# Retention with its group norm finished on GpSimd and ScalarE, other PSUM slots, and the modulation rows spread anew

## The chip, the cores and the metric

The kernel runs on one NeuronCore of a Trainium2 chip. Its engines work in parallel, each through its own instructions in order, and wait for each other through semaphores: TensorE (PE in the profile) multiplies matrices, VectorE (DVE) and ScalarE (ACT) work on tiles of 128 partitions, GpSimd (POOL) does small and odd work, and SyncE (SP) issues most of the DMAs. [...] The metric is the device time of one execution in microseconds (us). The kernel before takes 2175.5 us (median of 3 runs, 2174.44 to 2175.85).

## The reference

One decoder block on a sequence of 1024 tokens of width 1024, all in float32. What matters here is the retention: four heads, each with keys of 256 and values of 512, in chunks of 128 tokens, whose output is normed over its 512 values and gated.

```python
def step(state, inp):
    qi, ki, vi = inp
    s = jnp.einsum('bhid,bhjd->bhij', qi, ki) * inner_decay[None]
    o = (jnp.einsum('bhij,bhje->bhie', s, vi)
         + jnp.einsum('bhid,bhde->bhie', qi, state) * q_decay[None, :, :, None])
    state = (state * chunk_decay[None, :, None, None]
             + jnp.einsum('bhjd,bhje->bhde', ki * k_decay[None, :, :, None], vi))
    return state, o
...
mu = jnp.mean(ro, axis=-1, keepdims=True)
var = jnp.mean(jnp.square(ro - mu), axis=-1, keepdims=True)
ro = ((ro - mu) * lax.rsqrt(var + GN_EPS)).transpose(0, 2, 1, 3).reshape(B, S, RET_V_W)
ro = (ro * gn_g.astype(jnp.float32) + gn_b.astype(jnp.float32)).astype(h.dtype)
ret_out = (jax.nn.silu(rg) * ro) @ w_ret_out
...
mod = jax.nn.silu(c) @ w_ada[l] + b_ada[l]
sh1, sc1, g1, sh2, sc2, g2 = jnp.split(mod, 6, axis=-1)
```

Around it stand a dilated sliding-window attention, the merge of both branches, a projection, a squared-ReLU MLP and the norms. The vector mod scales and shifts the normed inputs (6 x 1024 values).

## The kernel before

All matmuls run in a split form. Each operand is cut into a high and a low half (`wh`, `wl`: ACT casts to the high half, DVE subtracts it to get the low one), and `mm3` (L203) issues three matmuls of 128x512 for each product: low weight by high input (L207), high by low (L209), high by high (L211). The first one of a product thus needs the low half of the weight.

The order of the instructions is written out by hand; there is no scheduler. `Steps` walks a list of steps. Each step has loads (weights or rows that go through a ring of three raw tiles, `wraw`) and a body. A body gets a function `ahead`, which prepares the loads of the next step: for a weight that is the ACT cast and the DVE subtraction of `split_w` (L197, L198), for a modulation row the DVE product of `mod_prep`. When the body calls it decides where these instructions stand in the order of ACT and DVE.

The stages that matter, in order:

1. `queries_keys` (about 180 to 600 us) runs 22 pairs of projections (`PAIRS`), each as seven block products (`ORDER`). The last six pairs have no rotation to do and are called light here. From product 116 on, `mod_turn` (L1248) computes rows of the modulation: it multiplies a row of `w_ada` with the conditioning vector and sums it (L1252, DVE, 128x1024), in a ring of two tiles (`cossin`) that SP refills (L1254). 32 rows are done this way, one in 16/7 calls; the calls go on in the next stage.
2. `values` (600 to 712 us) computes what is left of the retention's values. Its results go through the same three raw tiles (`vo`) and out by SP (`vd<-vo`, L1371).
3. The retention (712 to 980 us): 32 steps, `chunk(h, c)`, for four heads of eight chunks. The number g counts through. In each chunk PE computes, in this order, the state's update `kv` (six matmuls, not in chunk 7 of a head), some slices of a gate projection `rg` (below), the scores of the next chunk (`s_kt`: sT, and the transposed keys kT), the output `o` (from the state and from the scores), the transposes `oT` of the chunk before (`on_T`), and one more slice of `rg`.
   - DVE and ACT turn `kv` into the new state and its halves (L745, L749, L750), and sT and kT into the operands of the next chunk (sm, kh, kl and so on). kl, DVE's last but one of these, is what the next chunk's `kv` starts with.
   - `jit_qk` casts the queries and keys of chunk g + 2 on ACT (L616) and makes their low half on POOL (L617, 128x512).
   - The norm: DVE takes the statistics of `o` (bn_stats, L772, and L773), adds the epsilon (L774), POOL raises to the power -1/2 (L775), DVE multiplies with the decay (L776) and norms `o` to `onm` (L778).
   - `on_T` copies the transposes into `on` with four ACT copies.
   - `u_final` for the head before stands at the end of chunks 0 to 3 of heads 1 to 3: two ACT passes (L688) and one DVE product with the gate (L690), and the result out by SP.
4. A gate projection takes eight slices (one for each 128 of the contraction, six matmuls each). `RG` says how many slices each chunk gets, `rg_mm` issues them, `rg_out` applies Silu (L710). Three of a head's four gates are computed here, one comes from DRAM. The twelve weights are loads of the steps at c = 0, 2, 5.
5. The attention's first step, `att_step(0, 0)`, starts with a projection of keys (`ak`), whose weight is prepared by the last chunk's `ahead`.

`banks` divides PSUM: in the retention two gate pairs of two banks each (`ps_mm`) and four slots of one bank (`ps_s`), which kv, sT, kT, o and oT share.

## Time and profile before

| what | number |
|---|---|
| median of 3 runs | 2175.5 us |
| the profiled execution: its time | 2173.28 us |
| the profiled execution: its span, first to last instruction | 2171.3 us |
| mean granted TensorE clock | 0.999 |
| PE, DVE, ACT busy from 181 to 600 us, of 419 us | 419.0, 307.2, 123.3 |
| PE, DVE, ACT busy from 600 to 712 us, of 112 us | 108.8, 67.9, 46.4 |
| PE, DVE, ACT busy from 712 to 785 us, of 73 us | 71.2, 49.4, 34.9 |
| PE, DVE, ACT busy from 785 to 980 us, of 195 us | 194.9, 148.1, 105.8 |

How to read the lines of the profile that follow. A row of a group names the source line, the engine, the operation, out<-in by the program's names with the shapes, the count, then the busy time, the mean in ns, and the idle time of the engine before them with what ended it. A row of the timeline has the start in us from the span's start, the duration in us, then engine, line, operation, names and count; in brackets the idle time before it and who ended it. A row of waits names who waited for whom, the total in us, how often, and the longest. A row of stages has busy us (and instructions) of PE, its weight loads, DVE, ACT and POOL, then the granted clock, the DMA engines' share and GB/s. Matmuls of 128x512 last 0.39 us each but start every 0.226 us, so PE can lose some tenths of a us between two starts without an idle gap.

### The profile page before, as it was taken

Reading aid. Unit: us, or ns where it says so; the run is one execution under the profiler, and the core shown is the slowest. Engines: PE = TensorE matmul, PEld = TensorE weight load, DVE = VectorE, ACT = ScalarE, POOL = GpSimd, SP = SyncE. Lnnn points to the kernel's source line nnn. Section 1 sums busy time; section 2 is a strip of 40 time slices with the busy share of each in tenths; the row PEclk is TensorE's granted clock in tenths of the full one; section 3 lists DMA queues with packets and bytes.
Section 4 is the critical chain, followed back from the end, with each engine's and each line's share of the span. In section 5 each row is a group of like instructions: output and inputs, shape, how many; then the busy total and the mean of one; then the engine's idle time right before and its main releaser. Section 6 shows DMA issues by size and latency. Waiting matters only on the chain. (4 is left out here: it accounts for less than half of the span.)

```text
span 2171.3 us, 27289 instructions
## 1 busy us (share of the span) xinstructions
PE 2144.7 (99%) x10036; PEld 1782.4 (82%) x10036; DVE 1520.4 (70%) x2358; ACT 959.3 (44%) x1757; POOL 165.7 (8%) x199
## 2 busy tenths in 40 slices
PE   8999999999999999999999999999999999999998
PEld 6888888888887788888888888888778888888887
DVE  6886777777656677776667644677876665877855
ACT  5543322323334455556656625434454455533413
POOL 0001111100001112211110000001000000000003
PEclk9999999999999999999999999999999999999999
DMA  9859998835588744436877366653144435645322
GB/s 383 282 208 309 285 306 265 243 117 194 186 301 303 234 148 151 160 127 197 218 194 196 115 245 211 217 191 132 64 175 160 150 136 193 253 135 173 109 88 78
DMA packets 162674, 425.18 MB, mean 196 GB/s; under 512 B 28005, under 2 KB 55916, under 8 KB 159468
## 3 DMA queue, kind: packets, MB, share of 16 engines
q1 hardware_dynamic: 150264, 374.90, 48.3%
q0 software_dynamic: 9584, 48.24, 9.9%
q8 instruction: 79, 1.29, 0.2%
q10 hardware_dynamic: 2692, 0.30, 0.1%
q14 instruction: 55, 0.45, 0.1%
HBM read 324.13 MB, written 160.32 MB: 223 GB/s over the span
## 5 line engine op out<-in xcount | busy, mean ns | idle before, releaser
L207 PE MATMUL qap<-hh,qaw 128*128 128x512 f32 x264 | 102.7, 389 | 0.0
L209 PE MATMUL qap<-hl,qaw 128*128 128x512 f32 x264 | 102.7, 389 | 0.0
L211 PE MATMUL qap<-hh,qaw 128*128 128x512 f32 x264 | 102.7, 389 | 0.0
L617 POOL TENSOR_TENSOR j<-qk,j 128x512 fp32r<-128x512 f32 x32 | 42.8, 1338 | 454.8 <-ACT j L616 454.8
L2235 POOL TENSOR_TENSOR accnf<-accnf,sqnf 128x256 f32<-128x256 f32 (+1 forms) x18 | 16.6, 922 | 609.6 <-ACT sqnf L2231 609.6
L2339 ACT ACTIVATE a<-a 128x512 f32<-128x512 f32 x48 | 30.3, 631 | 72.8 <-DVE a L2338 71.3
L749 ACT CAST stateh<-state 128x512 fp32r<-128x512 f32 x54 | 32.9, 622 | 57.8 <-DVE state L745 55.7
L209 PEld LDWEIGHTS qap<-hl,qaw 128*128 128x128 f32 x264 | 49.5, 188 | 10.4
L211 PEld LDWEIGHTS qap<-hh,qaw 128*128 128x128 f32 x264 | 49.6, 188 | 10.3
L207 PEld LDWEIGHTS qap<-hh,qaw 128*128 128x128 f32 x264 | 49.5, 188 | 10.2
L2547 ACT CAST w2h<-w2s 128x512 fp32r<-128x512 f32 x36 | 22.4, 621 | 80.3 <-DVE w2s L2585 80.3
L264 DVE TENSOR_TENSOR fw<-w1r,fw 128x512 fp32r<-128x512 f32 x48 | 32.9, 688 | 33.6 <-ACT fw L254 33.6
L264 DVE TENSOR_TENSOR qaw<-wa,qaw 128x512 fp32r<-128x512 f32 x66 | 44.0, 687 | 9.4 <-ACT qaw L254 9.4
L2070 DVE TENSOR_TENSOR rwl<-rwl,rwh 128x1024 fp32r<-128x1024 f32 x25 | 30.2, 1221 | 29.0 <-ACT rwh L2100 29.0
L207 PE MATMUL fp<-h2h,fw 128*128 128x512 f32 x128 | 50.0, 390 | 0.0
L209 PE MATMUL fp<-h2l,fw 128*128 128x512 f32 x128 | 49.8, 389 | 0.0
L211 PE MATMUL fp<-h2h,fw 128*128 128x512 f32 x128 | 49.8, 389 | 0.0
L207 PE MATMUL roa<-rh,rwl 128*128 128x512 f32 x128 | 49.8, 389 | 0.0
L209 PE MATMUL roa<-rl,rwh 128*128 128x512 f32 x128 | 49.8, 389 | 0.0
L211 PE MATMUL roa<-rh,rwh 128*128 128x512 f32 x128 | 49.8, 389 | 0.0
L1603 ACT ACTIVATE P<-P,ng 128x128 f32<-128x128 f32 (+1 forms) x96 | 41.9, 438 | 17.6 <-DVE ng L1595 17.5
L292 DVE TENSOR_TENSOR qat<-qat,qap 128x512 f32<-128x512 f32 x22 | 15.1, 688 | 42.8 <-PE qap L211 35.8
(3089 smaller groups left out, 7187.8 us busy)
## 6 DMA issues: line engine op xcount, KB each, us to landing
cossin<-in_w_ada_dram SPq DMA_DIRECT2D x32, 512.0 KB, 3.5
v<-vd SPq DMA_DIRECT2D x32, 512.0 KB, 4.3
w1r<-in_w_ff_dram SPq DMA_DIRECT2D x32, 512.0 KB, 4.6
yt<-y POOLq DMA_DIRECT2D x24, 512.0 KB, 7.5
xsd<-as SPq DMA_DIRECT2D x24, 512.0 KB, 3.1
w2r<-in_w_ff2s_dram SPq DMA_DIRECT2D x24, 512.0 KB, 6.4
em<-in_w_ada_dram SPq DMA_DIRECT2D x16, 512.0 KB, 10.2
wrvs<-in_w_rv_dram POOLq DMA_DIRECT2D x16, 512.0 KB, 9.8
```

Of the source, the lines that this page charges most:

```text
L207: nc.tensor.matmul(o, wl, xh, start=first, stop=False, skip_group_check=skip)
L209: nc.tensor.matmul(o, wh, xl, start=False, stop=False, skip_group_check=skip)
L211: nc.tensor.matmul(o, wh, xh, start=False, stop=last, skip_group_check=skip)
L264: nc.vector.tensor_sub(t[:, 512:], src, fv(t[:, :512]))
L292: nc.vector.tensor_sub(u, u, b)
L617: nc.gpsimd.tensor_sub(t[:, 1], src, fv(t[:, 0]))
L749: nc.scalar.copy(sh1[:, i, :], st[:, i, :])
L1603: nc.scalar.activation(v, v, AF.Exp, bias=ng[:, blk:blk + 1], accum_out=st[:, g, blk, 2 + a:3 + a])
L2070: nc.vector.tensor_sub(lo, fv(lo), fv(hi))
L2235: (nc.vector if f == 7 else nc.gpsimd).tensor_add(G["acc", key], G["acc", key], sq)
L2339: nc.scalar.activation(o, o, AF.Relu)
L2547: nc.scalar.copy(hi, src)
```

## The change

- The norm's algebra: instead of the decay and its square (`CS_QD`, `CS_QD2`) the constants hold -1 and the epsilon divided by the decay's square. DVE adds that epsilon to the variance. POOL negates the mean, takes the power, and multiplies both. ACT applies scale and bias to `o` (one pass of 128x512 from PSUM) in place of DVE.
- `ahead(2)` of every chunk but the first moves from ahead of `s_kt` to behind the norm, and stands before `u_final`.
- PSUM in the retention: three gate halves of one bank (`ps_rg`) instead of two pairs of two, and five slots instead of four. The division of before comes back with the attention's first step.
- Each half of a gate has its own Silu, right behind the gate's last slice in `rg_mm`. The tiles of `on` are pairs of two, with two ACT copies instead of four.
- Head 3's slices are 4, 4, 4, 3, 3, 3, 3, 0. The weight of a gate is a load of the step in which its first slice stands.
- 22 modulation rows instead of 32 in `mod_turn`, one in 1.5 calls, so that all lie in the light pairs. The other ten are loads of the steps (0, 6), and (h, 4), (h, 5), (h, 6) of the heads 1 to 3.

```diff
-    def banks(single):
+    def banks(single, ret=False):
...
-        PS["n"] = 8 if single else 4
+        PS["n"] = 8 if single else 5 if ret else 4
...
+    def ps_rg(name):
+        return PS["p"].tile([P, 512], F32, tag="rg", bufs=3, name=name)
...
-            hd["on", h] = [etile(f"on{h}{e}") for e in range(4)]
+            hd["on2", h] = [R["p"].tile([P, 2, 1024], F32, tag="EO", bufs=4, name=f"on{h}{e}") for e in range(2)]
+            hd["on", h] = [hd["on2", h][e // 2][:, e % 2] for e in range(4)]
...
-        for e in range(4):
-            nc.scalar.copy(hd["on", h][e][:, c * C:(c + 1) * C], po[:, e, :])
+        for e in range(2):
+            nc.scalar.copy(hd["on2", h][e][:, :, c * C:(c + 1) * C], po[:, 2 * e:2 * e + 2, :])
...
-    RG = ((6, 2, 2, 3, 3, 3, 3, 2),) + ((3,) * NC,) * (H - 1)
+    RG = (6, 2, 2, 3, 3, 3, 3, 2), (3,) * NC, (3,) * NC, (4, 4, 4, 3, 3, 3, 3, 0)
...
-                hd["rgk"], hd["rgw"], hd["rgp"] = 0, hd["rgws"].pop(0), ps_mm("rg")
+                hd["rgk"], hd["rgw"], hd["rgp"] = 0, hd["rgws"].pop(0), [ps_rg(f"rg{i}") for i in range(2)]
...
-                hd["rgs"] = hd["rgp"]
+                i = hd["rgi"] = hd.get("rgi", -1) + 1
+                t = hd["srg", i // 3, i % 3] = etile(f"srg{i // 3}{i % 3}")
+                for j, ps in enumerate(hd["rgp"]):
+                    nc.scalar.activation(t[:, 512 * j:512 * j + 512], ps, AF.Silu)
...
-        rg_mm(1 if g == 0 else RG[h][c] - 1)
+        rg_mm(1 if g == 0 else max(RG[h][c] - 1, 0))
...
         if g == 0:
             jit_qk(2)
-        ahead(2)
+            ahead(2)
...
-        rg_mm(0 if g == 0 else 1)
+        rg_mm(min(RG[h][c], 1) if g > 0 else 0)
...
-        nc.vector.tensor_scalar(gr, ba[:, 1:2], ct[:, CS_QD2 + h:CS_QD2 + h + 1], GN_EPS, op0=ALU.mult, op1=ALU.add)
-        nc.gpsimd.tensor_tensor(gr, gr, mhalf[:, 0:1], op=ALU.pow)
-        nc.vector.tensor_mul(gr, gr, ct[:, CS_QD + h:CS_QD + h + 1])
+        nc.vector.tensor_scalar_add(gr[:, 0:1], ba[:, 1:2], ct[:, CS_EQ + h:CS_EQ + h + 1])
+        nc.gpsimd.tensor_tensor(gr[:, 2:3], ba[:, 0:1], ct[:, CS_NEG:CS_NEG + 1], op=ALU.mult)
+        nc.gpsimd.tensor_tensor(gr[:, 1:2], gr[:, 0:1], mhalf[:, 0:1], op=ALU.pow)
+        nc.gpsimd.tensor_tensor(gr[:, 2:3], gr[:, 1:2], gr[:, 2:3], op=ALU.mult)
         on = p.tile([P, DV], F32, tag="on", bufs=1, name=f"onm{h}{c}")
-        nc.vector.tensor_scalar(on, po, ba[:, 0:1], gr, op0=ALU.subtract, op1=ALU.mult)
+        nc.scalar.activation(on, po, AF.Identity, scale=gr[:, 1:2], bias=gr[:, 2:3])
         hd["o", h, c] = on
         rg_out(h, c)
+        if g > 0:
+            ahead(2)
         if h > 0 and c < 4:
             u_final(h - 1, (c,))
...
-    NV = 32
+    NV = 22
...
-        while turn["i"] < NV + 2 and 7 * turn["n"] > 16 * turn["i"]:
+        while turn["i"] < NV + 2 and 2 * turn["n"] > 3 * turn["i"]:
...
+    RGW, n = [], 0
+    for g in range(NG):
+        RGW += [g] * (n < 8 * len(RGW) + 1 <= n + RG[g // NC][g % NC])
+        n += RG[g // NC][g % NC]
+    late_mods = iter(range(G1 + NV, 48))
...
-                      ([wsplit(io["w_rg"][3 * h + (0, 2, 5).index(c)])] if c in (0, 2, 5) else []),
+                      ([wsplit(io["w_rg"][RGW.index(NC * h + c)])] if NC * h + c in RGW else []) +
+                      ([mod_load(next(late_mods))] if NC * h + c == 6 or h > 0 and c in (4, 5, 6) else []),
...
+            if pair == a == 0:
+                banks(False)
             ps = ps_mm(f"ak{pair}1{a}")
...
-        cst[:, CS_QD + h] = np.exp(lg * (i + 1))
-        cst[:, CS_QD2 + h] = np.exp(2 * lg * (i + 1))
+        cst[:, CS_NEG] = -1.0
+        cst[:, CS_EQ + h] = GN_EPS * np.exp(-2 * lg * (i + 1))
```

More of the change, by code (lines that the diff above doesn't have):

```diff
@@ L40 @@
 CS_KDEC = 128
-CS_QD = 132
-CS_QD2 = 136
+CS_NEG = 132
+CS_EQ = 136
 CS_ONE = 140
@@ L512, in etile @@
     def etile(name, dt=F32):
-        return R["p"].tile([P, 1024], dt, tag="E", bufs=12, name=name)
+        return R["p"].tile([P, 1024], dt, tag="E", bufs=4, name=name)
     y_d = [dram.tile([P, 4, 2, 512], F32, name=f"y{h}") for h in range(H)]
@@ L702, in rg_mm @@
             if hd["rgk"] == NK:
-                hd["rgs"] = hd["rgp"]
+                i = hd["rgi"] = hd.get("rgi", -1) + 1
+                t = hd["srg", i // 3, i % 3] = etile(f"srg{i // 3}{i % 3}")
+                for j, ps in enumerate(hd["rgp"]):
+                    nc.scalar.activation(t[:, 512 * j:512 * j + 512], ps, AF.Silu)
     def rg_out(h, c):
-        if "rgs" in hd:
-            e = {1: 0, 2: 0, 4: 1, 5: 1, 7: 2}[c]
-            hd["srg", h, e] = etile(f"srg{h}{e}")
-            nc.scalar.activation(hd["srg", h, e], flat(hd.pop("rgs")), AF.Silu)
         if c == 6:
@@ L767, in chunk @@
             on_T(*divmod(g - 1, NC))
-        rg_mm(0 if g == 0 else 1)
+        rg_mm(min(RG[h][c], 1) if g > 0 else 0)
         bn = p.tile([P, 6], F32, tag="bn", bufs=2, name=f"bn{h}{c}")
         ba = p.tile([P, 2], F32, tag="ba", bufs=2, name=f"ba{h}{c}")
-        gr = p.tile([P, 1], F32, tag="gr", bufs=2, name=f"gr{h}{c}")
+        gr = p.tile([P, 3], F32, tag="gr", bufs=2, name=f"gr{h}{c}")
         nc.vector.bn_stats(bn, po)
         nc.vector.bn_aggr(ba, bn)
-        nc.vector.tensor_scalar(gr, ba[:, 1:2], ct[:, CS_QD2 + h:CS_QD2 + h + 1], GN_EPS, op0=ALU.mult, op1=ALU.add)
-        nc.gpsimd.tensor_tensor(gr, gr, mhalf[:, 0:1], op=ALU.pow)
-        nc.vector.tensor_mul(gr, gr, ct[:, CS_QD + h:CS_QD + h + 1])
+        nc.vector.tensor_scalar_add(gr[:, 0:1], ba[:, 1:2], ct[:, CS_EQ + h:CS_EQ + h + 1])
+        nc.gpsimd.tensor_tensor(gr[:, 2:3], ba[:, 0:1], ct[:, CS_NEG:CS_NEG + 1], op=ALU.mult)
+        nc.gpsimd.tensor_tensor(gr[:, 1:2], gr[:, 0:1], mhalf[:, 0:1], op=ALU.pow)
+        nc.gpsimd.tensor_tensor(gr[:, 2:3], gr[:, 1:2], gr[:, 2:3], op=ALU.mult)
         on = p.tile([P, DV], F32, tag="on", bufs=1, name=f"onm{h}{c}")
-        nc.vector.tensor_scalar(on, po, ba[:, 0:1], gr, op0=ALU.subtract, op1=ALU.mult)
+        nc.scalar.activation(on, po, AF.Identity, scale=gr[:, 1:2], bias=gr[:, 2:3])
         hd["o", h, c] = on
         rg_out(h, c)
+        if g > 0:
+            ahead(2)
         if h > 0 and c < 4:
@@ L1427, in values @@
         R["state"] = R["p"].tile([P, 2, DV], F32, name="state")
-        banks(False)
+        banks(False, True)
     steps.add(first_values, manual=True)
```

## The prediction

> **What bounds the kernel now.** I read the page first, then the waits of TensorE, then the busy time by stage, and last the instructions of single retention chunks in order of time.

> ```profile
> span 2171.3 us, 27289 instructions
> PE 2144.7 (99%) x10036; PEld 1782.4 (82%) x10036; DVE 1520.4 (70%) x2358; ACT 959.3 (44%) x1757; POOL 165.7 (8%) x199
> ```

> TensorE (PE) works 99% of the span: 2171.3 - 2144.7 = 26.6 us are all that it idles. The change leaves every matmul in place, so a gain can only come out of those 26.6 us, while a new wait of PE is paid in full. PE's waits in the stages that are touched:

> ```profile
> PE vc L209 <- DVE vwl L1328: 1.9, 2, 1.5
> PE rg L207 <- DVE vr L1367: 1.1, 1, 1.1
> ...
> PE kv L207 <- ACT state L763: 0.9, 1, 0.9
> ...
> PE va L209 <- DVE vwlTrue L1330: 0.3, 1, 0.3
> ...
> PE va L207 <- ACT va L1376: 0.2, 1, 0.2
> PE kv L207 <- DVE kl L666: 0.2, 1, 0.2
> ```

> The values stage (vc, va) loses 2.4, the start of the retention (rg, kv) 2.2. In the rest of the retention PE hardly waits, but the other engines are near their limit there. One chunk with all kinds of work (head 1, chunk 1; VectorE is DVE, ScalarE is ACT, GpSimd is POOL):

> ```profile
> 795.23 1.22 DVE L198 TENSOR_TENSOR raw_5684l<-raw,raw_5684h 128x1024 fp32r<-128x1024 f32 x1 [0.25 <-ACT raw_5684h L197]
> ...
> 797.55 0.69 DVE L772 BATCH_NORM_STATS2 bn<-o 128x6 f32<-128x512 f32 x1
> 798.28 0.18 DVE L773 BATCH_NORM_AGGREGATE ba<-bn 128x2 f32<-128x6 f32 x1
> ...
> 799.74 0.16 DVE L776 TENSOR_TENSOR gr<-gr,ct 128x1 f32<-128x1 f32 x1 [1.03 <-POOL gr L775]
> 800.01 0.81 DVE L778 TENSOR_SCALAR onm<-o,ba,gr 128x512 f32<-128x512 f32 x1
> 800.74 1.22 DVE L690 TENSOR_TENSOR on<-on,srg 128x1024 f32<-128x1024 f32 x1
> 801.87 1.28 DVE L745 SCALAR_TENSOR_TENSOR state<-state,kv 128x512 f32<-128x512 f32 x2
> ...
> 805.63 0.69 DVE L772 BATCH_NORM_STATS2 bn<-o 128x6 f32<-128x512 f32 x1
> ...
> 794.15 1.04 ACT L197 CAST raw_5684h<-raw 128x1024 fp32r<-128x1024 f32 x1
> ...
> 798.37 1.55 ACT L688 ACTIVATE on<-on,gnt 128x512 f32<-128x512 f32 x2
> ...
> 797.91 1.30 POOL L617 TENSOR_TENSOR j<-qk,j 128x512 fp32r<-128x512 f32 x1 [7.75 <-ACT j L616]
> ...
> 789.02 0.39 PE L207 MATMUL kv<-v,kl 128*128 128x512 f32 x1
> ...
> 797.66 0.39 PE L207 MATMUL kv<-v,kl 128*128 128x512 f32 x1
> ...
> 799.03 0.61 PE L207 MATMUL rg<-hh,raw_5445l 128*128 128x512 f32 x2
> ...
> 806.62 0.39 PE L207 MATMUL kv<-v,kl 128*128 128x512 f32 x1
> ```

> PE needs 797.66 - 789.02 = 8.64 us for a chunk. DVE takes its work in order, and its round from one bn_stats to the next takes 805.63 - 797.55 = 8.08. So DVE has 0.6 us of room in the chunks that also finish the head before (u_final, chunks 0 to 3 of heads 1 to 3). Write D for the start of bn_stats. The next chunk's kv starts 1.0 after it here (806.62), and cannot start before D - 0.1, since kl is made just ahead of bn_stats.

> **The new chain of the norm.** Removed from DVE: the 0.16 and the 0.81 (L776, L778). Added: two products of 128x1 on POOL, around the power, and a pass of 512 with scale and bias on ACT. POOL starts on none of the three before the low half of j is done, at D + 1.66 (797.91 + 1.30). No row shows a product of 128x1 on POOL:

> ```profile
> L775 POOL TENSOR_TENSOR gr<-gr,ct 128x1 f32<-128x1 f32 x32 | 17.5, 546 | 15.2 <-DVE gr L774 15.2
> ...
> L376 POOL TENSOR_TENSOR nf1rs<-nf1rs,ct 128x2 f32<-128x2 f32 x1 | 0.7, 708 | 0.0
> ...
> L2906 POOL MEMSET const-uint8-127<- 128x1 uint8 x1 | 0.1, 117 | 0.0
> ...
> 649.41 0.60 ACT L1362 ACTIVATE vo<-va 128x512 fp32r<-128x512 f32 x1 [4.44 <-DMA vd<-vo]
> ```

> The second element of a power costs 708 - 546 = 162 ns, so 384 ns are there without it. I take 0.39 for a product; the ends are 0.12 (the memset) and 0.55 (the power). The ACT pass has the form of L688, also with two scale and bias vectors, 1.55 for two: I take 0.82 with its handover, with 0.60 (L1362, from PSUM without them) as the low end. The normed chunk is then ready at D + 1.66 + 0.39 + 0.55 + 0.39 + 0.07 + 0.82 = D + 3.9. PE wants it for the transposes a whole chunk later, so by itself this is hidden. What stands behind it is not.

> [...]

> **The split of the next weights.** In chunks after the first, the call of ahead moves from before s_kt to behind the norm. On ACT, in order, the high half (1.04) now stands behind the norm's pass, and DVE's low half (1.22) behind the high half: ready at D + 3.9 + 1.0 + 1.2 = D + 6.1. The first matmul of a gate uses the low half. An ordinary chunk (head 0, chunk 3) shows when PE would ask:

> ```profile
> 748.42 0.70 DVE L772 BATCH_NORM_STATS2 bn<-o 128x6 f32<-128x512 f32 x1 [0.70 <-PE o L211]
> ...
> 748.47 1.29 POOL L617 TENSOR_TENSOR j<-qk,j 128x512 fp32r<-128x512 f32 x1 [5.85 <-ACT j L616]
> ...
> 751.43 0.39 PE L207 MATMUL rg<-hh,raw_5357l 128*128 128x512 f32 x1
> ```

> PE reaches the gate's matmuls 3.0 after D. POOL is free at D + 1.34 here, which puts the low half at D + 5.8. So a gate that begins with the first slice after kv waits 2.8. Eleven gates begin inside the retention, by the order of the built program:
> - Four as in this row (head 0 chunk 5, and chunk 0 of heads 1, 2, 3): 4 x 2.8 = 11.2.
> - Head 0, chunk 2. The chunk before is short and DVE late in it:

> ```profile
> 733.45 0.69 DVE L772 BATCH_NORM_STATS2 bn<-o 128x6 f32<-128x512 f32 x1
> ...
> 734.81 0.39 PE L207 MATMUL rg<-hh,raw_5357l 128*128 128x512 f32 x1
> ```

> Without the split ahead of it (794.15 to 795.23 + 1.22 - 1.0 = 1.3 us of delay) bn_stats moves to 732.1, the low half to 738.2, and the gate from 734.81 to there: 3.4, the kv waits of 0.9 and 0.2 already counted in.
> - Head 3, chunk 2, whose eight-slice gates end a chunk earlier: D + 6.1 against kv at D + 1.0 and its 1.37 (799.03 - 797.66): 3.8 with handover.
> - Three with the second slice (chunk 5 of heads 1 and 2, chunk 4 of head 3). They follow u_final chunks, where kv comes at D - 0.1 (next part); PE asks at D - 0.1 + 1.37 + 1.36 = D + 2.6: 3 x 3.5 = 10.5.
> - Two begin with the last slice of a chunk and wait for nothing.
> - After the last chunk, the first attention weights are behind the norm too, and head 3's gates now end one chunk earlier, so no gate covers it:

> ```profile
> 979.13 0.70 DVE L772 BATCH_NORM_STATS2 bn<-o 128x6 f32<-128x512 f32 x1 [2.58 <-PE o L211]
> ...
> 979.28 0.71 PE L207 MATMUL rg<-hh,raw_7401l 128*128 128x512 f32 x2
> ```

> PE would start the keys at D + 0.15 (979.28, where the gate's last slice stands today). POOL has no j here and starts when the mean is there (798.28 + 0.18, D + 0.91): D + 0.95 + 1.33 + 0.07 + 0.82 + 1.0 + 1.2 = D + 5.4. Wait 5.3.

> **The u_final chunks.** Their two ACT passes (1.55) now stand behind the norm's, and DVE's product (1.22) behind these: it ends at D + 3.9 + 1.5 + 1.2 = D + 6.6, where DVE goes on to the states (0.1 before the product's end). From there to the next bn_stats it needs 805.63 - 801.87 = 3.76. The round becomes 10.3, or 11.25 where a split stands between (chunk 1), against PE's 8.64. For heads 1 and 2, from D of chunk 0 with kv 1.0 behind it: bn_stats at 10.3, 21.55, 31.85, 42.15; kv after chunks 1 to 4 cannot start before 10.2, 21.45, 31.75, 42.05, where PE is ready at 9.65, 18.85, 30.1, 40.4. Waits 0.55 + 2.6 + 1.65 + 1.65 = 6.45, twice: 12.9. Head 3 has four slices in three of these chunks, 1.36 more for PE, and its waits for splits cover the rest: 0.1.

> **The rest.** Rows of the modulation leave the values stage:

> ```profile
> 650.65 1.22 DVE L1252 SCALAR_TENSOR_TENSOR cossin<-cossin,cb 128x1024 f32<-128x1024 f32 x1
> ...
> vd<-vo SPq DMA_DIRECT2D x16, 512.0 KB, 10.1
> cossin<-in_w_ada_dram SPq DMA_DIRECT2D x15, 512.0 KB, 3.5
> ```

> Fifteen loads of 512 KB go from there, and with them, I take it, the slow landing (10.1) that holds ACT 4.44 (L1362 above) and then vwl: -2.4. The light pairs:

> ```profile
> 496.00:600.00 104.00, 104.00 (x461) 86.11 (x460) 72.96 (x112) 32.83 (x55) 0.00 (x0) 1.00 0.53 190
> ```

> A row comes there every 1.5 products instead of every 2.3: some 8 more in these 104 us, 10 of DVE's free 31, with loads two rows ahead. On SP each of these loads waits until DVE has used the row two before, and the weights and results behind it wait along; the weights are for two pairs on (a product is 12 matmuls of 104 / 461 = 0.226, a pair seven products, 19 us). I take 0; if that cover fails, 8 x 1.2. Ten rows in the retention stand behind bn_stats in chunks where ACT is the slower or nothing is late, loaded a chunk or more ahead: 0, at most 1.2 each. The later u_final sends its results later, and SP's fetches behind them are three chunks early: 0.

> The rg wait of 1.1 stays: the first gate bank is still the one that the values stage reads last. The third gate half is released by a Silu of half a gate, the fifth slot moves the wait for the state's read from o to oT; both 0, and 0.6 (512 on ACT, as L1362) a gate if ACT were late with them. Fewer, larger ACT copies save ACT time that nothing waits for.

> **Sum.** 11.2 + 3.4 + 3.8 + 10.5 + 5.3 + 12.9 + 0.1 - 2.4 = +44.8 on the profiled execution's 2173.28 (2171.3 the span, 2.0 around it): 2218.1. The median of the runs, 2175.5, is 2.2 above that execution, so I forecast 2220. With the cheap ends of product and pass each chain is 0.76 shorter: ten waits and 5.5 of the rounds, 13 less. With 0.55 a product, 6 more. So +32 to +51, or 2207 to 2226.

> **Rivals.**
> - The rounds do not bind, only the splits are late (DVE's 0.97 taken off and PE's own waits leave room): no 12.9, and the three second slices cost 2.8 - 1.36 = 1.4 each: 11.2 + 3.4 + 2.8 + 4.3 + 5.3 - 2.4 = +24.6, 2200. For it: DVE's load falls. Against: it waits in order for ACT. 22%.
> - PE's clock falls in the long waits. The first matmuls show what that is: eight take 3.58 (10.92 to 14.50), the next eight 1.87.

> ```profile
> 10.92 3.78 PE L866 MATMUL av<-wv0wh,hh 128*128 128x512 f32 x8 [1.70 <-ACT hh L410]
> 14.50 2.03 PE L866 MATMUL av<-wv0wh,hl 128*128 128x512 f32 x8
> ```

> Six waits of 3.4 or more at 1.7 each add 10: 2230. No wait inside the stages is long enough today to tell. 10%. [...]
> - The other side: DVE's relief decides and the late splits are hidden. Then the waits of vc, va (2.4), of kv (1.1) and some 1 us of smaller ones come off, -4.5: 2171. In the ordinary chunk it would need the norm's pass done by D + 3.0 - 1.0 - 1.2 = D + 0.8, from which point on each late 1 us costs about 10 us over the ten places; POOL's j alone ends at D + 1.34. 5%.
> - The gain and a few late splits cancel, within 0.2% (4.4 us, about what a measurement of this kernel can tell): 5%.

> **Chances.** The forecast with its ends 58%. Slower 58 + 22 + 10 = 90%, same 5%, faster 5%. The range runs from just under the first rival to just past the second: 2198 to 2232.

> **What would show it.** PE waiting for L201's low half at ten places by 2.8 to 5.3; kv waiting for kl 0.5 to 2.6 in chunks 1 to 4 of heads 1 and 2; POOL's products near 0.39; the norm's pass ending at D + 3.9; no vwl wait. Wrong would be it if ACT starts the split before the norm ends, or if kv starts on time in heads 1 and 2.

## The result, and the profile after

The changed kernel takes 2223.86 us (median of 5 runs, 2221.92 to 2228.47), the kernel before 2175.85 beside it (5 runs, 2174.44 to 2179.1). The ratio is 1.0223, with a 95% interval of 1.0208 to 1.0238: 48 us are lost. The profiled execution took 2221.92, its span is 2220.1. Its page begins:

```profile
span 2220.1 us, 27320 instructions
...
PE 2160.2 (97%) x10036; PEld 1790.0 (81%) x10036; DVE 1495.3 (67%) x2304; ACT 979.5 (44%) x1737; POOL 182.4 (8%) x263
```

The span grew by 48.8. PE now idles 2220.1 - 2160.2 = 59.9 instead of 26.6, which is 33.3 more. The other 15.5 are longer busy time of the same 10036 matmuls. These two parts have to be explained apart from each other. First the idle part, by PE's waits from the light pairs to the first attention keys (400 to 1060 us; who waited for whom, total, times, longest):

```profile
PE kv L210 <- DVE kl L669: 5.0, 6, 0.9
PE ak L210 <- DVE raw_8110l L201: 4.9, 1, 4.9
PE rg L210 <- DVE raw_5342l L201: 3.6, 1, 3.6
...
PE oT L681 <- DVE state L748: 2.7, 4, 0.7
...
PE rg L210 <- DVE raw_5344l L201: 2.5, 1, 2.5
...
PE rg L210 <- DVE raw_7549l L201: 1.8, 1, 1.8
PE rg L210 <- DVE vr L1373: 0.8, 1, 0.8
PE qap L210 <- DVE qat L296: 0.7, 1, 0.7
PE vc L212 <- DVE vwlFalse L1334: 0.3, 1, 0.3
```

Ten rows of this view end at L201, the low half of a weight: the keys with 4.9 and nine gates, from 3.6 down to 1.8 (three of the nine rows are shown, the rest lie between), 23.3. Together 28.2. The rounds of u_final cost 5.0 (kv) and 2.7 (oT), 7.7. The values stage waits 0.3 where it waited 2.4, the start of the retention 0.8 where it waited 2.2, and a wait of 0.7 came up in the light pairs. That is 28.2 + 7.7 - 2.1 - 1.4 + 0.7 = 33.1 of the 33.3.

The chain ahead of an ordinary gate (head 0, chunk 5) in order of time; D, the start of bn_stats, is 758.21:

```profile
758.21 0.70 DVE L775 BATCH_NORM_STATS2 bn<-o 128x6 f32<-128x512 f32 x1 [0.70 <-PE o L214]
...
759.63 0.19 POOL L778 TENSOR_TENSOR gr<-ba,ct 128x1 f32<-128x1 f32 x1
759.95 0.54 POOL L779 TENSOR_TENSOR gr<-gr,ct 128x1 f32<-128x1 f32 x1
760.57 0.19 POOL L780 TENSOR_TENSOR gr<-gr 128x1 f32<-128x1 f32 x1
760.79 0.78 ACT L782 ACTIVATE onm<-o,gr 128x512 f32<-128x512 f32 x1
761.47 1.03 ACT L200 CAST raw_5344h<-raw 128x1024 fp32r<-128x1024 f32 x1
762.54 1.22 DVE L201 TENSOR_TENSOR raw_5344l<-raw,raw_5344h 128x1024 fp32r<-128x1024 f32 x1 [2.67 <-ACT raw_5344h L200]
763.82 0.73 PE L210 MATMUL rg<-hh,raw_5344l 128*128 128x512 f32 x2 [2.45 <-DVE raw_5344l L201]
...
764.85 0.62 PE L214 MATMUL rg<-hh,raw_5344h 128*128 128x512 f32 x2
```

From the product on each row starts as the one above it ends, within 0.15: power, product, norm pass, high half, low half, gate. The high half follows the norm's pass on ACT without a pause. The low half is done at 763.76, D + 5.55. PE asked at 763.82 - 2.45 = 761.37, D + 3.2.

The busy part is mostly the clock. The same two matmuls of a gate behind two waits of the same length, one wait of 2.45 (above, 763.82) and one of 2.44:

```profile
789.60 1.01 PE L210 MATMUL rg<-hh,raw_5728l 128*128 128x512 f32 x2 [2.44 <-DVE raw_5728l L201]
790.40 1.06 PE L212 MATMUL rg<-hl,raw_5728h 128*128 128x512 f32 x2
791.26 1.06 PE L214 MATMUL rg<-hh,raw_5728h 128*128 128x512 f32 x2
```

A pair of matmuls takes 0.86 from start to start here (790.40 to 791.26), where it takes 0.46 behind the other wait. By stretches (PE, its weight loads, DVE, ACT and POOL busy, then the granted clock): two stretches of 3.41 us for the first wait, two for the second, one behind the wait of the keys, and the end of the stage:

```profile
759.16:762.57 3.41, 2.20 (x10) 1.48 (x8) 0.43 (x3) 2.83 (x5) 1.25 (x4) 1.00 0.02 5
762.57:765.98 3.41, 2.17 (x9) 1.80 (x10) 3.32 (x5) 1.22 (x2) 0.00 (x0) 1.00 0.29 71
786.47:789.88 3.41, 0.97 (x5) 0.51 (x4) 1.56 (x2) 1.82 (x3) 0.00 (x0) 1.00 0.00 0
789.88:793.29 3.41, 3.41 (x9) 2.68 (x9) 2.16 (x4) 1.22 (x2) 0.00 (x0) 0.50 0.67 223
1026.70:1032.00 5.30, 5.29 (x12) 4.13 (x13) 1.10 (x1) 0.00 (x0) 0.00 (x0) 0.50 0.59 199
...
985.00:1040.00 55.00, 48.19 (x214) 39.16 (x214) 30.48 (x61) 27.07 (x54) 10.98 (x19) 0.91 0.34 115
```

The granted clock is 0.50 behind the second wait and behind that of the keys, and 1.00 behind the first; the last section shows in what the two waits differ. Over the end of the retention and the first keys (985 to 1040) its mean is 0.91.

### The profile page after: what moved, and what is told of

The parts are those of the page before. It is cut to its first block, busy times and chain, and to the rows that moved or that the text cites. A ratio compares the mean times of both kernels' runs of the same rounds, so it can differ in the third digit from the quotient of the medians.

```text
span 2220.1 us, 27320 instructions
## 1 busy us (share of the span) xinstructions
PE 2160.2 (97%) x10036; PEld 1790.0 (81%) x10036; DVE 1495.3 (67%) x2304; ACT 979.5 (44%) x1737; POOL 182.4 (8%) x263
## 3 DMA queue, kind: packets, MB, share of 16 engines
q8 instruction: 79, 1.29, 0.3%
## 5 line engine op out<-in xcount | busy, mean ns | idle before, releaser
L212 PEld LDWEIGHTS qap<-hl,qaw 128*128 128x128 f32 x264 | 49.6, 188 | 10.1
L267 DVE TENSOR_TENSOR qaw<-wa,qaw 128x512 fp32r<-128x512 f32 x66 | 44.0, 685 | 10.1 <-ACT qaw L257 10.1
L1615 ACT ACTIVATE P<-P,ng 128x128 f32<-128x128 f32 (+1 forms) x96 | 41.9, 439 | 17.5 <-DVE ng L1607 17.5
L782 ACT ACTIVATE onm<-o,gr 128x512 f32<-128x512 f32 x32 | 24.9, 780 | 46.0 <-POOL gr L780 46.0
## 6 DMA issues: line engine op xcount, KB each, us to landing
v<-vd SPq DMA_DIRECT2D x32, 512.0 KB, 4.7
w1r<-in_w_ff_dram SPq DMA_DIRECT2D x32, 512.0 KB, 5.0
yt<-y POOLq DMA_DIRECT2D x24, 512.0 KB, 7.3
xsd<-as SPq DMA_DIRECT2D x24, 512.0 KB, 2.7
w2r<-in_w_ff2s_dram SPq DMA_DIRECT2D x24, 512.0 KB, 6.2
cossin<-in_w_ada_dram SPq DMA_DIRECT2D x22, 512.0 KB, 3.5
em<-in_w_ada_dram SPq DMA_DIRECT2D x16, 512.0 KB, 10.2
wrvs<-in_w_rv_dram POOLq DMA_DIRECT2D x16, 512.0 KB, 9.4
```

What stands on the lines that cost most here:

```text
L212: nc.tensor.matmul(o, wh, xl, start=False, stop=False, skip_group_check=skip)
L267: nc.vector.tensor_sub(t[:, 512:], src, fv(t[:, :512]))
L782: nc.scalar.activation(on, po, AF.Identity, scale=gr[:, 1:2], bias=gr[:, 2:3])
L1615: nc.scalar.activation(v, v, AF.Exp, bias=ng[:, blk:blk + 1], accum_out=st[:, g, blk, 2 + a:3 + a])
```

## The experiments

Times are medians; the kernel before ran beside each group. The first row is the result above.

| kernel | us | ratio to before, 95% interval |
|---|---|---|
| as changed | 2223.86 | 1.0223 [1.0208, 1.0238] |
| changed, ahead early again | 2199.8 | 1.0116 [1.0099, 1.0133] |
| changed, u_final ahead of the norm pass | 2210.05 | 1.0160 [1.0144, 1.0176] |
| changed, both of these orders | 2177.87 | 1.0009 [0.9999, 1.0018] |
| changed, waits filled with surplus matmuls | 2212.04 | 1.0169 [1.0154, 1.0184] |
| changed, norm finished on DVE | 2192.53 | 1.0083 [1.0069, 1.0098] |
| before, ahead late | 2191.03 | 1.0076 [1.0061, 1.0091] |
| before, rows as changed | 2180.11 | 1.0023 [1.0013, 1.0032] |
| before, rows mostly in head 0 | 2174.65 | 1.0003 [0.9994, 1.0012] |
| before, rows in head 0, slower pace | 2173.55 | 0.9995 [0.9986, 1.0004] |
| changed, both orders, gates and rows moved | 2173.43 | 0.9995 [0.9986, 1.0004] |

### The split early again

```diff
         if g == 0:
             jit_qk(2)
-            ahead(2)
+        ahead(2)
...
         rg_out(h, c)
-        if g > 0:
-            ahead(2)
```

> The changed kernel with one part undone: every chunk calls ahead before s_kt again, the norm stays on POOL and ScalarE. Theory (the late splits make the waits for the low half, 28.2 us of PE's idle time, and the half-speed matmuls behind them, about 11 us): both go, the waits of the u_final rounds (kv 5.0, oT 2.7) stay: 2223.9 - 28.2 - 11.1 - 3 = 2181, between 2178 and 2187. Rival 1 (the rounds were only disturbed by the late splits and come out even without them): 2174. Rival 2 (the norm on POOL and ScalarE is the cost, not the place of the split): above 2210.

Measured: 2199.8, 24 less than as changed, but 19 more than my number and between the rivals. The gates' waits for low halves are gone. In their place the rounds got worse. Waits and instructions in order of time of this kernel (head 1, chunk 3):

```profile
PE kv L210 <- DVE kl L669: 16.1, 10, 3.3
...
810.79 1.23 DVE L694 TENSOR_TENSOR on<-on,srg 128x1024 f32<-128x1024 f32 x1 [3.52 <-ACT on L692]
814.51 1.22 DVE L467 SCALAR_TENSOR_TENSOR raw<-raw,cb 128x1024 f32<-128x1024 f32 x1
...
816.90 0.50 PE L210 MATMUL kv<-v,kl 128*128 128x512 f32 x1 [2.11 <-DVE kl L669]
```

DVE waits 3.52 for ACT's passes of u_final, which stand behind the norm; then come the states, and the row of the modulation (L467), which the early ahead puts in front of kl. As changed, the same row and the low half fill DVE's wait for ACT. Of the 19, 8.4 are these longer waits (16.1 in place of 7.7). Another 8 are, by estimate, the clock, which my number had at full speed: this trace has 17.1 us at half the granted clock, and PE works for 16.1 of them. So the late split costs the gates, but it also covered work of DVE, and undoing it alone takes that cover away. The theory of the gates holds; my assumption that the rounds would stay as they were is refuted, and so is the rival in which they would come out even.

### Both orders

```diff
+        if h > 0 and c < 4:
+            u_final(h - 1, (c,))
         nc.scalar.activation(on, po, AF.Identity, scale=gr[:, 1:2], bias=gr[:, 2:3])
...
-        if h > 0 and c < 4:
-            u_final(h - 1, (c,))
```

together with the edit above.

> The changed kernel with ahead before s_kt in every chunk and with u_final ahead of the norm's ScalarE pass, so that VectorE's product in u_final no longer waits behind the norm. Theory (the rounds are late because VectorE waits in order for ScalarE): the waits of kv and oT in chunks 1 to 4 of the later heads go too, and what is left is the values stage's gain of 2.4 and some of the smaller waits: 2172, between 2169 and 2176. Rival (the rounds are bound by the sum of the work, the order does not matter): as with the early split alone, 2181.

Measured: 2177.87, 46 of the 48 us back, 2 above my range. DVE's product of u_final now starts 2.3 behind bn_stats (794.68 to 796.95) and waits 0.97 instead of 3.52:

```profile
794.68 0.69 DVE L775 BATCH_NORM_STATS2 bn<-o 128x6 f32<-128x512 f32 x1
796.95 1.23 DVE L694 TENSOR_TENSOR on<-on,srg 128x1024 f32<-128x1024 f32 x1 [0.97 <-ACT on L692]
...
PE rg L210 <- ACT srg L710: 3.3, 3, 1.7
...
PE ak L210 <- DVE raw_8053l L201: 1.3, 1, 1.3
```

What is left is a wait for Silus (3.3, none as changed), the keys, 1.6 for kl, and 1.9 in the light pairs, which neither order touches. In these orders the whole change, the norm on POOL and ACT included, costs nothing that this run can tell; the interval leaves room for 4 us.

### u_final first, the split still late

The second edit alone, with ahead left behind the norm.

> The changed kernel with u_final ahead of the norm's ScalarE pass, ahead still behind the norm. Theory (the waits of kv 5.0 and oT 2.7 in the rounds come from VectorE's product waiting in order behind the norm's pass): these 7.7 and some 1.5 of slower first matmuls go, the ten waits for the low half stay, those that follow the rounds a little longer: 2223.9 - 9 = 2215, between 2211 and 2219. Rival (what the rounds give back is taken by the next gate's wait in full): 2221 or more.

Measured: 2210.05, 14 less than as changed and 1 below my range. The waits of kv and oT in the rounds are gone, and the gates that follow the rounds wait less, not longer:

```profile
PE ak L210 <- DVE raw_8114l L201: 4.9, 1, 4.9
PE rg L210 <- DVE raw_7453l L201: 3.8, 1, 3.8
...
PE rg L210 <- DVE raw_6245l L201: 1.2, 1, 1.2
```

Chunk 5 of heads 1 and 2 waits 1.2 instead of 2.7, I take it because the late product of u_final had delayed the chain there too. Only chunk 2 of head 3 waits longer (3.8 instead of 2.8).

### The waits filled

Surplus matmuls ahead of nine gates and of the keys, in place of PE's idle time; the split is as late as before.

```diff
                 hd["rgk"], hd["rgw"], hd["rgp"] = 0, hd["rgws"].pop(0), [ps_rg(f"rg{i}") for i in range(2)]
+                for i in range(FILL.get(g, 0)):
+                    nc.tensor.matmul(hd["rgp"][0], fill_w, fill_x, start=i == 0, stop=i == FILL[g] - 1)
...
```

> The changed kernel, with surplus matmuls (128x512, their result is overwritten) ahead of nine gates and of the first attention keys, as many as fit into the measured wait (6 to 14, and 19): PE is busy while it waits, the splits are as late as before. Theory (waits are followed by matmuls at half the clock, 2.3 to 5.3 us long in seven places, 11 us in all): granted clock 1.00 in the retention, 11 us less, 2213, between 2210 and 2217. Rival 1 (the longer busy time of PE comes from something else than its idling): 2224, clock as it was. Rival 2 (the surplus matmuls delay the gates): above 2224.

Measured: 2212.04, 11.8 less, as the clock's theory has it, and both rivals fall. The same stretch of this kernel, at a clock of 1.00, and the keys in order of time:

```profile
985.00:1040.00 55.00, 53.64 (x256) 43.66 (x255) 33.51 (x56) 29.09 (x52) 11.63 (x19) 1.00 0.43 148
...
1013.97 4.60 PE L1855 MATMUL ak<-hh 128*128 128x512 f32 x19
1019.08 0.72 PE L210 MATMUL ak<-hh,raw_8190l 128*128 128x512 f32 x2 [0.51 <-DVE raw_8190l L201]
```

19 matmuls whose result nobody uses (in the same way ahead of the keys) stand where PE idled 4.86, and the first two real ones behind them take 0.72, as behind the wait without a slow clock. So some 12 of the 15.5 of longer busy time are the clock's fall after idling. (The two profiled executions differ by only 8.7, 2221.92 and 2213.21, so the size is rough.) The granted clock gives the size a second time: the trace as changed has 27.3 us at half the clock between 735 and 1033, the filled one has none. PE works for 25.6 of them and so loses, by estimate, 12.8. The rest I did not isolate; the first two matmuls behind a wait show 0.73 where later ones show 0.62 (763.82 and 764.85 above), which over the 20 waits for low halves, kl and the states is some 2.

### The two halves of the chain: place and engine

Before, with the call of ahead moved behind the norm in the chunks after the first, and nothing else:

> The kernel before, with only the call of ahead moved behind the norm in the chunks after the first; the norm is finished on VectorE as before. Theory (the low half stands behind the norm, wherever that is finished, and the norm on VectorE is done 1.5 us sooner than on POOL and ScalarE): waits of about 1.2 at the ordinary gates, 1.9 in chunk 2 of head 0, 0.5 at three second slices, 2.3 at the first keys, no longer rounds and little loss of clock: 2175.5 + 10.5 = 2186, between 2181 and 2194. Rival 1 (the place of the split alone costs nearly all of it): 2212 or more. Rival 2 (with the norm on VectorE the split still comes in time): 2176.

As changed, with the norm finished on DVE and POOL's power alone:

```diff
-        nc.gpsimd.tensor_tensor(gr[:, 2:3], ba[:, 0:1], ct[:, CS_NEG:CS_NEG + 1], op=ALU.mult)
...
-        nc.gpsimd.tensor_tensor(gr[:, 2:3], gr[:, 1:2], gr[:, 2:3], op=ALU.mult)
...
-        nc.scalar.activation(on, po, AF.Identity, scale=gr[:, 1:2], bias=gr[:, 2:3])
+        nc.vector.tensor_scalar(on, po, ba[:, 0:1], gr[:, 1:2], op0=ALU.subtract, op1=ALU.mult)
```

> The changed kernel with one part undone: the norm is finished on VectorE (subtract and multiply in one pass), with POOL's power alone. The split stays behind the norm, slots, gate halves and rows stay as changed. Theory (the two engines that finish the norm only lengthen the chain ahead of the split, and make the rounds late): near the kernel before with the move alone, 2191.0, less 2.4 of the values stage, more 3 for head 3's gates of eight slices and its earlier end: 2192, between 2187 and 2198. Rival (slots, gate halves or rows cost something of their own): above 2200.

Measured: 2191.03 and 2192.53, both within their ranges. The late place alone costs 15.5, and with the norm on DVE the whole rest of the change (gate halves, rows and the slots in PSUM, which the matmuls write, were not taken apart) adds next to nothing to it. Of the kernel before with the move, then of the changed one with the norm on DVE, the waits:

```profile
PE rg L207 <- DVE raw_5445l L198: 1.9, 1, 1.9
```

```profile
PE rg L210 <- DVE raw_6229l L201: 0.4, 1, 0.4
```

An ordinary gate waits 1.8 or 1.9 instead of 2.4; my expectation had 1.2, too little. The chunk 5 gates wait 0.4 instead of 2.7, there is no wait for kl or the states left, and two waits are followed by a slow clock instead of seven. So neither the place of the split nor the engines of the norm make the 48 by themselves: the place costs 15.5, the norm's end on POOL and ACT in that place another 31.

### The rows alone

```diff
-    NV = 32
+    NV = 22
...
-        while turn["i"] < NV + 2 and 7 * turn["n"] > 16 * turn["i"]:
+        while turn["i"] < NV + 2 and 2 * turn["n"] > 3 * turn["i"]:
...
+                      ([mod_load(next(late_mods))] if NC * h + c == 6 or h > 0 and c in (4, 5, 6) else []),
```

on the kernel before.

> The kernel before with the modulation rows alone changed: 22 in the light pairs and the values stage at the faster pace, ten in the retention in the places of the change. Theory (the rows' loads made the waits of vc and va; in the retention, with ahead before s_kt, a row is three VectorE instructions of 1.5 us ahead of kl): 2.4 gained, and where two of a head's three rows fall into its u_final rounds, which have 0.6 of room, about 0.9 lost each, 5 in all: 2178, between 2174 and 2182. Rival 1 (the rows cost nothing there): 2173. Rival 2 (the waits of vc and va do not come from the rows): 2180 or more, with these waits still there.

Measured: 2180.11, about 5 slower, within the range but for other reasons in part:

```profile
PE kv L207 <- DVE kl L666: 4.8, 4, 1.6
PE qap L207 <- DVE qat L293: 2.4, 3, 1.5
...
PE vc L209 <- DVE vwlFalse L1328: 0.3, 1, 0.3
```

The values stage does give back its waits (vc from 1.9 to 0.3), but the faster pace puts 2.4 of new ones into the light pairs, and one row in each of three rounds costs 1.5.

### Versions that might beat the kernel before

The ten rows elsewhere, `NC * h + c in (4, 5, 6, 7, 8, 9, 14, 15, 22, 23)`:

> As the run with the rows alone, the ten rows in other places: six in the chunks of head 0, which have no u_final, and two each late in heads 1 and 2. Theory (the values stage's gain is real and a row is hidden where VectorE has no product of u_final): 2175.5 - 2.4 = 2173, between 2171 and 2175.5, faster than before. Rival (VectorE has no room there either): 2177 or more.

The same with a row every 1.75 products in the light pairs (`4 * turn["n"] > 7 * turn["i"]`):

> As the kernel before with 22 rows and the ten others mostly in head 0, with the pace in the light pairs between the old and the new one (a row every 1.75 products). Theory (the new waits of qap, 1.6, come from the rows' pace, and at this pace neither they nor those of vc and va appear): 2174.7 - 1.6 = 2173, between 2171.5 and 2174.5. Rival (the rows reach the values stage again and bring back its waits): 2175.

And the changed kernel with both orders, these places of the rows, and three slices a chunk in head 3:

> The changed kernel with ahead before s_kt, u_final ahead of the norm's ScalarE pass, head 3's gates at three slices a chunk again and the ten rows in other chunks (six in head 0, two each late in heads 1 and 2). Theory (what the run with both orders undone still waits for, 1.7 for a Silu and 1.3 for the first keys in head 3, comes from the gates that end a chunk earlier, and 1.0 for kl from the rows): 2177.9 - 4 = 2174, between 2172 and 2176.5. Rival (the norm on POOL and ScalarE delays the Silus in any case): 2177 to 2179.

Measured: 2174.65, 2173.55 and 2173.43, against 2174.87 beside the first and 2174.41 beside the others. The first is at the rival's side of its range, as the waits of the light pairs stay:

```profile
PE qap L207 <- DVE qat L293: 1.6, 3, 1.0
```

At the slower pace these are gone and vc does not come back, as expected; a wait of 0.3 for va does. The last two are each 1 us faster in the median, but their intervals, 0.9986 to 1.0004, include no change. So there is a form of the change whose cost these runs cannot tell from none, and none here that is shown to gain.

## Why the prediction was right

The forecast was 2220, the median is 2223.86. The direction and the cause, the split behind the new chain of the norm, came out as said. That the sum came so close is luck, since two errors nearly cancel: the waits were forecast 11.7 too long (44.8 against 33.1), and the 15.5 of longer busy time, some 12 of it the clock's loss, were not in the sum; the clock stood in a rival.

- Low halves late, ten places: forecast 11.2 + 3.4 + 3.8 + 10.5 + 5.3 = 34.2, measured 28.2. The ten places are the right ones. By place: the four ordinary gates 2.4 to 2.5 for 2.8, chunk 2 of head 0 3.6 for 3.4, chunk 2 of head 3 2.8 for 3.8, the second slices 2.7, 2.7 and 1.8 for 3.5, the keys 4.9 for 5.3. The mis-sized term is POOL's product of 128x1: I took 0.39 between 0.12 and 0.55, and it is 0.19 in both places (759.63 and 760.57 above). Two of them make the chain 0.4 shorter; handovers of about 0.1 between POOL's rows, which I had left out, take a part of it back. (For one element a partition the traces have 0.19 on POOL here and 0.16 on DVE, L776 of the kernel before.) The ordinary low half is ready at D + 5.55 instead of D + 5.8, and PE asks at D + 3.2 instead of D + 3.0. Why chunk 4 of head 3 waits as little as 1.8 I did not follow up.
- The rounds: forecast 12.9 + 0.1, measured 7.7, all in heads 1 and 2. The mechanism is the one described, as u_final ahead of the norm's pass takes these waits away. The size fails by the same product first. Starts of bn_stats in head 1 of the changed kernel:

```profile
796.19 0.69 DVE L775 BATCH_NORM_STATS2 bn<-o 128x6 f32<-128x512 f32 x1
...
805.91 0.69 DVE L775 BATCH_NORM_STATS2 bn<-o 128x6 f32<-128x512 f32 x1
...
816.58 0.69 DVE L775 BATCH_NORM_STATS2 bn<-o 128x6 f32<-128x512 f32 x1
...
826.31 0.69 DVE L775 BATCH_NORM_STATS2 bn<-o 128x6 f32<-128x512 f32 x1
...
837.02 0.69 DVE L775 BATCH_NORM_STATS2 bn<-o 128x6 f32<-128x512 f32 x1
```

  The rounds are 9.72, 10.67, 9.73 and 10.71, where I had 10.3, 11.25, 10.3 and 10.3 (the last one is taken up below, with POOL's product). By my own rule these starts, 9.72, 20.39, 30.12 and 40.83 after the first, would make kv wait 0, 2.0, 1.1 and 2.1, so 5.2 in place of 6.45. (For the low end of the range I took 5.5 off the rounds; the same rule gives 6.0.) The rule holds: kv of chunk 5 starts 39.68 after kv of chunk 1 (836.90 and 797.22), where four chunks of 8.64 take 34.56, so 5.1 are lost. Of these, 3.85 stand as idle time (7.7 for two heads); the remainder is among the longer busy time, in the matmuls that run slowly behind each wait.
- The values stage: forecast -2.4, measured -2.1, and the run with the rows alone shows that the waits go with the rows. The light pairs, forecast 0, wait 0.7. The start of the retention, left at 1.1 for rg, waits 0.8.
- Ten rows in the retention at 0: most of their time is hidden in this kernel, where they stand in DVE's wait for ACT. But the row in chunk 3 of heads 1 and 2 holds up POOL's product (last section) and makes each of these two rounds 1.0 longer. With ahead in its old place one in each of three rounds costs 1.5.
- The rival of the clock: its mechanism is shown, its size about (10 forecast, 11.8 measured), but not its condition. I counted six waits of 3.4 or more at 1.7 each. No run shows 3.4 as the length that it takes: two of this kernel's waits are that long (3.6 and 4.9), and five shorter ones, 1.8 to 2.8, were followed by a slow clock as well. Nor does the trace of before show that the first matmuls, from which I had the 1.7, ran at a lower clock: its record of the granted clock begins at 14.56, with 1.00. Behind the seven waits here the half clock costs, by the estimate of 12.8 above, 1.8 each.
- The rival without rounds (2200) falls, since kv and oT do wait. So do the two that had the change hidden or cancelled. The kernel with the early split lands at 2199.8 by another way: there kv waits 16.1 and no gate waits for its weight.

## What to carry to other kernels

When the last step of a chain moves to another in-order engine, list what stands behind it on that engine and on the one it left, and put the work that others wait for (the next weights, the earlier result) ahead of the new step: here the same norm on POOL and ACT costs 48 us in one order and 2, not told from none, in another. An order may also be hiding work, so undoing half of a change can show a loss that neither version has. Where PE is the bound, price the longer waits above their length: here 17 of the 22 waits of 2.0 us or more were followed by a slow clock (next section), and 28.2 of idle time at the late weights cost some 12 again through it.

## What the hardware showed beside this

How long PE idled where its clock fell. In the twelve profiles of this case, from 400 to 2150 us, I counted PE's waits and those followed within 4 us by at least three matmuls of 512 more than 0.38 us apart:

| wait, us | waits | slow clock behind it |
|---|---|---|
| 0.7 to 1.7 | 103 | 0 |
| 1.7 to 2.0 | 14 | 4 |
| 2.0 to 2.8 | 14 | 9 |
| 3.3 to 4.9 | 8 | 8 |

Between 1.7 and 2.8 the length does not decide: 2.44 was followed by half the clock, the 2.45 shown above was not.

Some instructions of POOL and DVE took longer beside each other. Seven of the 32 first products took 1.17 to 1.25 instead of 0.19, each of them beside a modulation row on DVE (L467, 128x1024; the durations' least, median and largest in ns, then head 1, chunk 3 of the changed kernel, and a row of its chunk 1):

```profile
L778 POOL TENSOR_TENSOR gr<-ba,ct x32: 180/190/1247, 724.5 to 1022.6; 128x1 f32<-128x1 f32 x32
...
826.67 1.30 POOL L620 TENSOR_TENSOR j<-qk,j 128x512 fp32r<-128x512 f32 x1 [7.53 <-ACT j L619]
827.53 1.53 DVE L467 SCALAR_TENSOR_TENSOR raw<-raw,cb 128x1024 f32<-128x1024 f32 x1
827.93 1.17 POOL L778 TENSOR_TENSOR gr<-ba,ct 128x1 f32<-128x1 f32 x1
...
829.67 0.19 POOL L780 TENSOR_TENSOR gr<-gr 128x1 f32<-128x1 f32 x1
...
808.29 0.19 POOL L780 TENSOR_TENSOR gr<-gr 128x1 f32<-128x1 f32 x1
```

DVE's row takes 1.53 instead of 1.22 where POOL's j runs on into it (to 827.97 here), and POOL's product ends with it: in all seven the two ends lie within 0.06 of each other. The three rows of the retention beside which POOL runs none of these take 1.22. What holds the two engines up was not shown. This has a price: POOL's second product comes 0.98 later than two chunks before (829.67 is 3.36 behind bn_stats, 808.29 was 2.38 behind it), and the round from 826.31 is 10.71 long instead of 9.73.
